# Key parts written once and spread by three transfers, a float32 head norm, and new prices in the planner

## The chip, the cores and the metric

The kernel runs on one core of a Trainium2 chip. The metric is the device time of one launch in microseconds (us). Before the change it is 791.28 us, the median of three runs between 790.02 and 792.25.

## The reference, cut to what matters

One layer of an encoder over two request groups that share weights: 1,040 prompt rows (16 meta tokens and 1,024 frames) and 32 sample rows with a cache of 272 rows. All of it is in float32.

```python
h = _rmsnorm(x, g)
z = h @ w_in                       # 1024 x 4104: dq, dk, dv, fq, fk, fv, forget logits, gate
...
sd = einsum(qd, Kd) * scale - slopes * dist      # 4 heads, two maps each
ad = softmax(sd)[:, :, 0] - lam * softmax(sd)[:, :, 1]
od = _rmsnorm(ad @ Vd, subln_g, 1e-5) * (1.0 - lam_init)     # the head norm, over 128 columns
...
of = softmax(einsum(qf, Kf) * scale + Fq - Fk) @ Vf          # 8 heads of 64
y = x + (concat(od, of) * silu(gate)) @ w_out
```

The new key and value rows and the forget logarithms are outputs as well, and y gets a last RMS norm.

## The kernel before, in words

**Number format.** TensorE works on float16 pairs: each float32 operand is split in a high part and a remainder (`hi`, `lo`), and a product is three products of the parts.

**Pairs.** The work is cut into eight pairs p of 128 columns. Pairs 0 to 3 are the four differential heads, whose 128 key columns are the two maps of 64; pairs 4 to 7 hold two forgetting heads of 64 each. For each pair there are projections of values, keys and queries (`proj_tasks`, the products of L864, in three column groups of up to 416, four for pair 0), then scores (`unit_tasks`, L1268), softmax (minimum on VectorE L1282, exponential on ScalarE L1288), splitting of the probabilities (L1317 to L1339, L1350, L1356), a transpose by DMA (L1368) and the products with the values (L1380 to L1387). The gate projections (also L864, weights `Wg`) come behind all pairs in priority and fill TensorE while the softmax of the pairs runs. At the end comes the output projection (L1806).

**Keys.** A projected group lies transposed on 128 partitions (`zT`, L883), map 0 on partitions 0 to 63 and map 1 on 64 to 127. The tile `k` is `[128, 2, 2, columns]`: map, then high part or remainder. A score product contracts 128 partitions: the query's high part on one half, its remainder on the other, against the same key on both halves. So the key of a map has to stand on both halves of the partitions. GpSimd writes the high part of each map on its own half (L891, two instructions a group), GpSimd or VectorE the remainder (L896, two a group; GpSimd for the pairs in `K_POOL`), and then one transfer per map copies the half to the other one (L993, 268 KB each, on SyncE's queue).

**Head norm.** `fin_tasks` normalizes the output of a differential head over its 128 rows, 256 columns at a time: sixteen times, and four times with 32 columns for the sample rows. ScalarE writes the values `o` and their squares `q`. For 256 columns GpSimd rounds the squares to float32r (L1441) and subtracts (L295, tile `fq`), and TensorE sums them over the partitions by two float32r products with a matrix of 1/128 (L1449, L1450); for 32 columns it is one float32 product (L1452). ScalarE takes r = exp(-0.5 ln(s + eps)) (L1457, L1458), and a Newton step sharpens it: VectorE v = (s + eps) r (L1463), GpSimd v = v r (L1470), VectorE v = (v - 3) r (L1474) and out = o v (L1475). The constants' signs are folded into the gain.

**Order.** Nothing is ordered at run time. A planner (`Graph.order`) simulates the engines as queues: each task has an engine, a cost in ns, a priority, the tasks it depends on and the buffers it takes; whenever an engine is free it takes the task of the highest priority whose buffers are there. The order that comes out is written down as each engine's instruction order. So a cost in a task changes no instruction, but where it stands. `c_dve`, `c_pool`, `c_act` and `c_mm` give costs by columns, `c_ts` that of a GpSimd tensor_scalar; a transfer is done 1,600 ns (`LANDED`) after its bytes, priced by `move` per KB, have moved.

```python
    def c_dve(n, k=1):
        return k * (165.0 + 1.08 * n)
    def c_ts(n):
        return 240.0 + 1.05 * n
```

In the functions printed here, `add(engine, cost, function, priority, dependencies, acquired, used)` makes a task.

Of the kernel before, what the change touches and what calls it, by code (L numbers as in the profile page):

```python
# [9 lines left out]
F32 = mybir.dt.float32  # L10
# [25 lines left out]
COLD = 3400.0  # L36

TRANSPOSED = 2000.0
LANDED = 1600.0
LATE = 8  # L40
# [20 lines left out]
FIN_POOL = True  # L61
# [200 lines left out]
def tile_hymba(  # L262
# [43 lines left out]

    def c_ts(n):
        return 240.0 + 1.05 * n
# [301 lines left out]
    def spread_task(col_, prio, deps):  # L610
# [12 lines left out]
        td = add("pool", 370, fd, prio, list(deps) + [cn["id"]], [dh])  # L623
# [22 lines left out]
    def w_tasks(key, prio):  # L646

        x = "Wg" if key[0] == "g" and key[1] < LATE else "W"
# [184 lines left out]
    def proj_tasks(kind, p, prio, step=0.1):  # L833
# [13 lines left out]
        for gi, (c0, c1) in enumerate(groups):  # L847
# [40 lines left out]
            if kind == "k":  # L888
                def fh(z=zT, c0=c0, c1=c1):
                    for m, (a, b) in enumerate(((0, 64), (64, 128))):  # L890
                        pool.tensor_scalar(out=K[p]["t"][a:b, m, 0, c0:c1], in0=z()[a:b], scalar1=1.0, scalar2=1.0,  # L891
                                           op0=ALU.mult, op1=ALU.mult)

                def fl(z=zT, c0=c0, c1=c1):
                    for m, (a, b) in enumerate(((0, 64), (64, 128))):
                        (pool if p in K_POOL else dve).tensor_tensor(  # L896
                            out=K[p]["t"][a:b, m, 1, c0:c1], in0=z()[a:b], in1=K[p]["t"][a:b, m, 0, c0:c1], op=ALU.subtract)
                th = add("pool", 2 * c_ts(n), fh, pr - 0.05, [tz], [], [zh, K[p]["hold"]])
                tl = add("pool" if p in K_POOL else "dve", c_pool(n, 2) if p in K_POOL else c_dve(n, 2), fl, pr, [th], [], [zh, K[p]["hold"]])
# [52 lines left out]
            if kind == "g":  # L952
# [29 lines left out]
                t4 = add("dve", c_dve(n, 2), f5, pr, [t4], [], [eh, ph])  # L982
                gate_done[p, gi] = dma(lambda p=p, c0=c0, c1=c1, n=n, loc=loc: sp.dma_start(
                    out=gate_s[128 * p:128 * p + 128, c0:c1], in_=loc["e"][:, :n]), pr, [t4], [], [eh], kb=n / 2)
        if kind == "k":
            K[p]["dup"] = []
            for i in range(2):
                b = 64 * i
                a = 64 - b

                def fd(i=i, a=a, b=b):
                    t = K[p]["t"]
                    sp.dma_start(out=t[a:a + 64, i], in_=t[b:b + 64, i])  # L993
                K[p]["dup"].append(dma(fd, prio, K[p]["hi"] + K[p]["lo"], [], [K[p]["hold"]], kb=268))
# [244 lines left out]
    def unit_tasks(p, hd, gg, prio, bias, av):  # L1239
# [5 lines left out]
        for bi in range(2):  # L1245
# [6 lines left out]
            for m in maps:  # L1252
# [44 lines left out]
                t = add("dve", 300, fq, prio + 0.3, [te, cn["lam"]])  # L1297
                if p < 4 and m == 1:
# [3 lines left out]
                    t = add("pool", 300 + 1.0 * nk, fp, prio + 0.3, [t], [], [ph])  # L1302
# [96 lines left out]
    def fin_tasks(p, get, ah, dep, n, d0, prio, u=1.0, ug=1.0):  # L1399
# [43 lines left out]
        if n > 32:  # L1443
            t1 = add("pool", c_ts(n) + c_pool(n), fs, prio, [t1], [], [fh])
# [506 lines left out]
```

## Time and profile before

| | |
|---|---|
| median of three runs | 791.28 us |
| the profiled execution | 794.14 us, its span 792.4 us |
| mean granted TensorE clock | 0.936 of full speed |
| busy: TensorE, VectorE, ScalarE, GpSimd | 684.0, 633.8, 498.9, 435.3 us |

The profile is one execution. The span runs from the first instruction to the last; the profiled execution's own time is longer by what lies around it. PE is TensorE, PEld its weight load, DVE is VectorE, ACT ScalarE, POOL GpSimd, and SP SyncE, which issues the transfers. A line such as L891 is a line of the kernel before. In a group of instructions the busy time is a sum over the whole span, the mean is that of one instruction, and the idle time is that of the engine just ahead of them, with what ended it. The chain is followed back from the last instruction to whatever released each step.

### The profile page before, as it was taken

What the parts mean: (1) busy time and instruction counts of PE and PEld (TensorE: products, weight loads), DVE (VectorE), ACT (ScalarE), POOL (GpSimd) and SP (SyncE); (2) the same over time, 40 slices, a digit from 0 to 9 for tenths busy, and PEclk for the clock granted to TensorE, in tenths of its full rate; (3) what the DMA queues carried; (4) which work ended last, traced back from release to release, by engine and by line L of the source; (5) the groups of instructions that cost most, each with busy time, mean ns of one, the idle gap of its engine ahead of it and who ended that gap; (6) DMA issues with size and microseconds to landing.
All of it is one profiled execution on the core that took longest, in us unless ns stands there. A gap on an engine that the chain in (4) does not pass through costs nothing.

```text
span 792.4 us, 14862 instructions
## 1 busy us (share of the span) xinstructions
PE 684.0 (86%) x4967; PEld 453.1 (57%) x4967; DVE 633.8 (80%) x1665; ACT 498.9 (63%) x1140; POOL 435.3 (55%) x606
## 2 busy tenths in 40 slices
PE   4477989898898899999899989979998973599996
PEld 4355565565765566666566667657665752334443
DVE  5966789888977889998889988878488889847643
ACT  4753578468766566876677677858488585434432
POOL 1447444698956569986867466546565148610000
PEclk8588999999899999999999999999999997599999
DMA  8284444556745355536686897788774987987611
GB/s 234 69 172 97 91 134 52 87 113 89 127 90 125 63 124 118 111 79 138 142 138 137 147 177 166 144 145 157 157 245 96 191 197 146 212 220 233 195 54 54
DMA packets 235804, 108.28 MB, mean 137 GB/s; under 512 B 149984, under 2 KB 228136, under 8 KB 235728
## 3 DMA queue, kind: packets, MB, share of 16 engines
q1 hardware_dynamic: 235728, 107.34, 62.9%
q8 instruction: 39, 0.64, 0.3%
q14 instruction: 37, 0.30, 0.1%
HBM read 46.39 MB, written 21.87 MB: 86 GB/s over the span
## 4 chain that ended last, share of the span: by engine, by line
PE 32%; DVE 16%; DMA 9%; POOL 6%; issue 4%; ACT 2%; SPq 1%; DVEq 0%; POOLq 0%; ACTq 0%
PE pj L864 13%; PE pj L1806 12%; DMA raw<-in_w_in_dram 4%; DMA arena<-arena 3%; DVE arena L1282 3%; DVE arena L1339 2%; PE sc L1268 2%; DMA ckr<-in_cache_diff_k_dram 2%; POOL k L896 1%; PE av L1384 1%; DVE gr L975 1%; PE av L1385 1%; DVE mx L1424 1%; POOL k L891 1%; DVE ge L971 1%
## 5 line engine op out<-in xcount | busy, mean ns | idle before, releaser
L864 PE MATMUL pj<-hT,W 128*128 128x384 f16 (+4 forms) x1776 | 294.9, 320 | 12.7 <-DVE ge L976 5.7
L864 PEld LDWEIGHTS <-W 128*128 128x128 f16 x1776 | 175.2, 101 | 110.7 <-issue 22.2
L1282 DVE CUSTOM_DVE_ANT_0 arena<-sc,G,stats 128x400 f32<-128x400 f32 (+9 forms) x224 | 128.6, 589 | 15.6 <-PE sc L1268 6.6
L1288 ACT ACTIVATE arena<-arena,stats 128x656 f32<-128x656 f32 (+7 forms) x128 | 99.9, 781 | 28.7 <-DVE stats L1282 26.8
L864 PE MATMUL pj<-hT,Wg 128*128 128x416 f16 (+2 forms) x576 | 97.6, 322 | 5.0 <-DVE ge L976 3.3
L1268 PE MATMUL sc<-k,q 128*128 128x400 f16 (+9 forms) x448 | 90.2, 311 | 8.1 <-DVE stats L1282 5.7
L1806 PE MATMUL pj<-hT,W 128*128 128x512 f16 (+4 forms) x440 | 95.6, 373 | 1.2 <-DVE W L1778 1.2
L618 POOL TENSOR_SCALAR diag<-ident,stats 128x128 bf16<-128x128 f32 x51 | 27.0, 529 | 99.9 <-ACT W L1773 48.5
L864 PEld LDWEIGHTS <-Wg 128*128 128x128 f16 x576 | 56.5, 101 | 35.5 <-issue 5.6
L1806 PEld LDWEIGHTS <-W 128*128 128x128 f16 (+2 forms) x440 | 41.7, 98 | 53.3 <-issue 8.6
L1384 PE MATMUL av<-arena,vn 128*128 128x128 f16 x288 | 43.3, 235 | 24.0 <-DMA arena<-arena 16.7
L1268 PEld LDWEIGHTS <-q 128*128 128x128 f16 x448 | 40.3, 100 | 29.5 <-issue 13.5
L1339 DVE SCALAR_TENSOR_TENSOR arena<-arena,stats 128x128 f16<-128x128 f32 (+4 forms) x80 | 50.5, 670 | 4.7 <-ACT arena L1331 3.7
L1356 POOL TENSOR_TENSOR arena<-arena 128x16 f16<-128x16 f32 (+3 forms) x48 | 36.3, 779 | 20.4 <-ACT arena L1350 20.3
L1323 POOL TENSOR_TENSOR arena<-arena 128x16 f16<-128x16 f32 (+7 forms) x56 | 44.1, 812 | 2.0 <-ACT arena L1317 1.9
L1385 PE MATMUL av<-arena,vn 128*128 128x128 f16 x288 | 43.4, 235 | 0.0
L883 ACT ACTIVATE zT<-pj 128x416 f32<-128x416 f32 (+4 forms) x50 | 22.5, 449 | 31.9 <-PE pj L864 30.8
L1385 PEld LDWEIGHTS <-vn 128*128 128x128 f16 x288 | 30.5, 106 | 18.7 <-issue 17.3
L1334 POOL TENSOR_SCALAR arena<-arena,stats 128x128 f16<-128x128 f32 (+2 forms) x32 | 22.9, 729 | 29.9 <-PE sc L1270 14.1
L1384 PEld LDWEIGHTS <-vn 128*128 128x128 f16 x288 | 30.6, 106 | 14.6 <-DVE mx L1424 7.7
L663 ACT ACTIVATE W<-raw 128x1024 bf16<-128x1024 f32 x24 | 25.2, 1050 | 19.8 <-DMA raw<-in_w_in_dram 19.6
L891 POOL TENSOR_SCALAR k<-zT 64x416 f16<-64x416 f32 (+4 forms) x50 | 30.1, 603 | 12.6 <-ACT zT L883 10.5
(318 smaller groups left out, 1566.5 us busy)
## 6 DMA issues: line engine op xcount, KB each, us to landing
raw<-in_w_in_dram SPq DMA_DIRECT2D x32, 512.0 KB
arena<-in_x_prompt_dram SPq DMA_DIRECT2D x16, 512.0 KB
k<-k SPq DMA_DIRECT2D x16, 268.0 KB
G<-G_t SPq DMA_DIRECT2D x8, 520.0 KB
mix_s<-mx SPq DMA_DIRECT2D x32, 128.0 KB
out_dram<-arena SPq DMA_DIRECT2D x16, 256.0 KB
arena<-mix_s SPq DMA_DIRECT2D x7, 512.0 KB
arena<-gate_s SPq DMA_DIRECT2D x7, 512.0 KB
```

Of the source, the lines that this page charges most:

```text
L618: pool.tensor_scalar(out=loc["d"], in0=ident, scalar1=col_, scalar2=1.0, op0=ALU.mult, op1=ALU.mult)
L864: mm(out, (W["hi"], W["hi"], W["lo"])[w][:, k, :], (hTh, hTl, hTh)[w][:, k, c0:c1], start=i == 0, stop=i == 23)
L891: pool.tensor_scalar(out=K[p]["t"][a:b, m, 0, c0:c1], in0=z()[a:b], scalar1=1.0, scalar2=1.0, op0=ALU.mult, op1=ALU.mult)
L1268: mm(s[:, :b - a], q, K[p]["t"][:, m, x, a:b], start=x == 0, stop=x == 1 and not mask)
L1282: dve.tensor_tensor_reduce(out=A(ph, nk)[:, a:b], in0=loc["s"][:, :b - a], in1=bl["t"][:, o + a:o + b], scale=Q[p]["tau"], scalar=3e38 if ...
L1288: te = add("act", c_act(nk) + 125, lambda ph=ph, nk=nk, mn=mn, sm=sm: act.activation(out=A(ph, nk), in_=A(ph, nk), func=AF.Exp, scale=-1.0 ...
L1323: (pool if on_pool else dve).tensor_tensor(out=A16(w, o, o + b - a), in0=x[:, a:b], in1=A16(w, h, h + b - a), op=ALU.subtract)
L1339: dve.scalar_tensor_tensor(out=A16(w, o, o + b - a), in0=x[:, a:b], scalar=rk, in1=A16(w, h, h + b - a), op0=ALU.mult, op1=ALU.subtract)
L1356: pool.tensor_tensor(out=A16(w, o, o + b - a), in0=x[:, a:b], in1=A16(w, h, h + b - a), op=ALU.subtract)
L1384: mm(out, vn[:, j, 128 * hd:128 * hd + 128], hi, start=j == 0, stop=False)
L1385: mm(out, vn[:, j, 128 * hd:128 * hd + 128], lw, start=False, stop=False)
L1806: mm(d, a, b, start=k == 0 and i == 0, stop=k == 7 and i == len(ops) - 1)
```

## The change

The diff, cut to its core:

```diff
+PORT = 200.0
+PORT_P = 150.0
-LATE = 8
+G_AT = (250, 260, 270, 280, 290, 300, 310, 320)
-FIN_POOL = True
...
+    def c_dvs(n, k=1):
+        return k * (PORT + 165.0 + 1.08 * n)
     def c_ts(n):
-        return 240.0 + 1.05 * n
+        return PORT_P + 240.0 + 1.05 * n
...
-        td = add("pool", 370, fd, prio, list(deps) + [cn["id"]], [dh])
+        td = add("pool", 370 + PORT_P, fd, prio, list(deps) + [cn["id"]], [dh])
...
                 def fh(z=zT, c0=c0, c1=c1):
-                    for m, (a, b) in enumerate(((0, 64), (64, 128))):
-                        pool.tensor_scalar(out=K[p]["t"][a:b, m, 0, c0:c1], in0=z()[a:b], scalar1=1.0, scalar2=1.0,
-                                           op0=ALU.mult, op1=ALU.mult)
+                    pool.tensor_scalar(out=K[p]["t"][:, 0, 0, c0:c1], in0=z(), scalar1=1.0, scalar2=1.0, op0=ALU.mult, op1=ALU.mult)
 
                 def fl(z=zT, c0=c0, c1=c1):
-                    for m, (a, b) in enumerate(((0, 64), (64, 128))):
-                        (pool if p in K_POOL else dve).tensor_tensor(
-                            out=K[p]["t"][a:b, m, 1, c0:c1], in0=z()[a:b], in1=K[p]["t"][a:b, m, 0, c0:c1], op=ALU.subtract)
-                th = add("pool", 2 * c_ts(n), fh, pr - 0.05, [tz], [], [zh, K[p]["hold"]])
-                tl = add("pool" if p in K_POOL else "dve", c_pool(n, 2) if p in K_POOL else c_dve(n, 2), fl, pr, [th], [], [zh, K[p]["hold"]])
+                    (pool if p in K_POOL else dve).tensor_tensor(
+                        out=K[p]["t"][:, 0, 1, c0:c1], in0=z(), in1=K[p]["t"][:, 0, 0, c0:c1], op=ALU.subtract)
+                th = add("pool", c_ts(n), fh, pr - 0.05, [tz], [], [zh, K[p]["hold"]])
+                tl = add("pool" if p in K_POOL else "dve", c_pool(n) if p in K_POOL else c_dvs(n), fl, pr, [th], [], [zh, K[p]["hold"]])
...
-            K[p]["dup"] = []
-            for i in range(2):
-                b = 64 * i
-                a = 64 - b
-
-                def fd(i=i, a=a, b=b):
-                    t = K[p]["t"]
-                    sp.dma_start(out=t[a:a + 64, i], in_=t[b:b + 64, i])
-                K[p]["dup"].append(dma(fd, prio, K[p]["hi"] + K[p]["lo"], [], [K[p]["hold"]], kb=268))
+            def fd1():
+                t = K[p]["t"]
+                sp.dma_start(out=t[64:128, 1], in_=t[64:128, 0])
+                sp.dma_start(out=t[0:64, 1], in_=t[64:128, 0])
+
+            def fd0():
+                t = K[p]["t"]
+                sp.dma_start(out=t[64:128, 0], in_=t[0:64, 0])
+            d1 = dma(fd1, prio, K[p]["hi"] + K[p]["lo"], [], [K[p]["hold"]], kb=536, move=2.25, n=2)
+            K[p]["dup"] = [dma(fd0, prio, [d1], [], [K[p]["hold"]], kb=268, move=2.25), d1]
...
-        def fs():
-            loc["qh"], loc["ql"] = [T([128, n], F32R, f"fq{i}") for i in range(2)]
-            pool.tensor_scalar(out=loc["qh"], in0=loc["q"], scalar1=1.0, scalar2=1.0, op0=ALU.mult, op1=ALU.mult)
-            sub_r(pool, loc["ql"], loc["q"], loc["qh"])
-        if n > 32:
-            t1 = add("pool", c_ts(n) + c_pool(n), fs, prio, [t1], [], [fh])
-
         def f2():
             loc["s"] = PSUM("sc")
-            if n > 32:
-                mm(loc["s"][:, :n], onesr, loc["qh"], start=True, stop=False)
-                mm(loc["s"][:, :n], onesr, loc["ql"], start=False, stop=True)
-            else:
-                mm(loc["s"][:, :n], onesm, loc["q"], start=True, stop=True)
-        t2 = add("pe", 2 * c_mm(n), f2, prio, [t1, cn["c"]], [sh], [fh])
+            mm(loc["s"][:, :n], onesm, loc["q"], start=True, stop=True)
+        t2 = add("pe", 4 * c_mm(n), f2, prio, [t1, cn["c"]], [sh], [fh])
...
         def f5():
-            v, r0 = loc["v"], loc["r"]
-            loc["mx"] = T([128, n], F32, x + "mx", RINGS[x + "mx"])
-            (pool if FIN_POOL else dve).tensor_tensor(out=v, in0=v, in1=r0, op=ALU.mult)
-
-        def f6():
-            v, r0 = loc["v"], loc["r"]
-            dve.scalar_tensor_tensor(out=v, in0=v, scalar=-3.0, in1=r0, op0=ALU.add, op1=ALU.mult)
-            dve.tensor_tensor(out=loc["mx"], in0=loc["o"], in1=v, op=ALU.mult)
-        t5 = add("pool" if FIN_POOL else "dve", c_pool(n) if FIN_POOL else c_dve(n), f5, prio, [t4], [mh], [fh])
-        t5 = add("dve", c_dve(n, 2), f6, prio, [t5], [], [fh, mh])
+            pool.tensor_tensor(out=loc["o"], in0=loc["o"], in1=loc["r"], op=ALU.mult)
+            pool.tensor_tensor(out=loc["v"], in0=loc["v"], in1=loc["r"], op=ALU.mult)
+
+        def f6():
+            loc["mx"] = T([128, n], F32, x + "mx", RINGS[x + "mx"])
+            dve.scalar_tensor_tensor(out=loc["mx"], in0=loc["v"], scalar=-3.0, in1=loc["o"], op0=ALU.add, op1=ALU.mult)
+        t5 = add("pool", c_pool(n, 2), f5, prio, [t4], [], [fh])
+        t5 = add("dve", c_dvs(n), f6, prio, [t5], [mh], [fh])
```

The high part and the remainder of both maps are now written by one instruction each, into the place of map 0. Two transfers then copy partitions 64 to 127, which are map 1, into the place of map 1 on both halves; after they have landed, a third copies map 0 over partitions 64 to 127 of its own place. The head norm uses one float32 product for all sizes, and its last step is out = (v r - 3) (o r).

Not shown are the other places where the planner's price of a task is changed: `c_dvs` (200 ns more an instruction) replaces `c_dve` for the gates' last two VectorE steps (L975, L976), for the sum of the two maps (L1312) and for the remainders of the probabilities on VectorE (L1323, L1339); the reciprocals of L1292 get 80 ns more; the scaling of L1300 is priced by `c_ts`, as are the others of that kind. `G_AT` replaces the formula for the gates' priorities, which gave 250 to 320 as well, and with `LATE` at 8 every gate weight already used the ring `Wg`.

## Rows read from the trace of the kernel before

**Rows 1.** Page of the profile, part 1: busy us, share of the span, instructions by engine.

```profile
PE 684.0 (86%) x4967; PEld 453.1 (57%) x4967; DVE 633.8 (80%) x1665; ACT 498.9 (63%) x1140; POOL 435.3 (55%) x606
```

**Rows 2.** Stretches: from:to, length, PE, PEld, DVE, ACT, POOL busy us (count), clock, DMA, GB/s.

```profile
100.00:410.00 310.00, 280.22 (x2127) 192.68 (x2126) 270.76 (x743) 215.68 (x524) 226.44 (x307) 0.96 0.55 107
410.00:580.00 170.00, 159.37 (x1281) 110.55 (x1280) 138.63 (x402) 117.97 (x267) 100.71 (x158) 0.99 0.80 153
580.00:640.00 60.00, 56.12 (x451) 38.24 (x449) 52.25 (x158) 46.68 (x108) 21.68 (x31) 0.97 0.78 193
640.00:690.00 50.00, 25.38 (x223) 18.68 (x221) 45.15 (x102) 31.34 (x60) 37.10 (x31) 0.78 0.79 160
```

**Rows 3.** Timeline of TensorE, the last gate projection: start, length, what.

```profile
644.64 1.57 PE L864 MATMUL pj<-hT,Wg 128*128 128x416 f16 x8
```

**Rows 4.** Waits of TensorE from 640 to 690 us: total us, times, longest.

```profile
PE av L1384 <- DMA arena<-arena: 10.6, 5, 4.2
PE av L1384 <- DVE mx L1424: 7.3, 2, 4.1
```

**Rows 5.** Page, part 4: the chain that ended last, by engine and by line.

```profile
PE 32%; DVE 16%; DMA 9%; POOL 6%; issue 4%; ACT 2%; SPq 1%; DVEq 0%; POOLq 0%; ACTq 0%
PE pj L864 13%; PE pj L1806 12%; DMA raw<-in_w_in_dram 4%; DMA arena<-arena 3%; DVE arena L1282 3%; DVE arena L1339 2%; PE sc L1268 2%; DMA ckr<-in_cache_diff_k_dram 2%; POOL k L896 1%; PE av L1384 1%; DVE gr L975 1%; PE av L1385 1%; DVE mx L1424 1%; POOL k L891 1%; DVE ge L971 1%
```

**Rows 6.** Groups by line, the key parts: count | busy us, mean ns | idle before.

```profile
L896 POOL TENSOR_TENSOR k<-zT,k 64x272 f16<-64x272 f32 (+2 forms) x36 | 34.3, 954 | 2.7
...
L891 POOL TENSOR_SCALAR k<-zT 64x416 f16<-64x416 f32 (+4 forms) x50 | 30.1, 603 | 12.6 <-ACT zT L883 10.5
...
L896 DVE TENSOR_TENSOR k<-zT,k 64x256 f16<-64x256 f32 (+4 forms) x14 | 8.4, 600 | 3.3 <-POOL k L891 3.1
```

**Rows 7.** Instructions of L891: min/median/max ns.

```profile
L891 POOL TENSOR_SCALAR k<-zT x50: 302/530/1982, 67.2 to 569.0; 64x416 f16<-64x416 f32 x16, 64x272 f16<-64x272 f32 x14, 64x384 f16<-64x384 f32 x14, 64x256 f16<-64x256 f32 x4
```

**Rows 8.** Instructions on tile fs: min/median/max ns.

```profile
L1441 POOL TENSOR_SCALAR fq<-fs x16: 394/406/1367, 132.9 to 405.2; 128x256 fp32r<-128x256 f32 x16
...
L1463 DVE SCALAR_TENSOR_TENSOR fs<-sc,fr x16: 401/421/426, 144.7 to 409.6; 128x256 f32<-128x256 f32 x16
...
L1474 DVE SCALAR_TENSOR_TENSOR fs<-fs,fr x16: 406/426/1569, 151.3 to 411.2; 128x256 f32<-128x256 f32 x16
L1475 DVE TENSOR_TENSOR mx<-ft,fs x16: 424/515/2237, 152.7 to 411.6; 128x256 f32<-128x256 f32 x16
```

**Rows 9.** Groups by line: the head norm, and float32 products of the warm-up.

```profile
L295 POOL TENSOR_TENSOR fq<-fs,fq 128x256 fp32r<-128x256 f32 x16 | 14.2, 888 | 1.3
...
L1470 POOL TENSOR_TENSOR fs<-fs,fr 128x256 f32<-128x256 f32 x16 | 13.5, 846 | 8.3 <-DVE fs L1463 8.1
L1475 DVE TENSOR_TENSOR mx<-ft,fs 128x256 f32<-128x256 f32 x16 | 13.4, 839 | 0.5
...
L1441 POOL TENSOR_SCALAR fq<-fs 128x256 fp32r<-128x256 f32 x16 | 11.0, 688 | 5.0 <-ACT fs L1435 4.8
...
L1474 DVE SCALAR_TENSOR_TENSOR fs<-fs,fr 128x256 f32<-128x256 f32 x16 | 10.8, 676 | 4.2 <-POOL fs L1470 4.1
...
L1864 PE MATMUL pj<-ident 128*128 128x128 f32 x48 | 7.5, 333 | 1.4 <-POOL eps L1855 1.4
```

**Rows 10.** Timeline of TensorE, one head norm's pair, then the next product.

```profile
164.98 0.36 PE L1449 MATMUL sc<-fq,onesr 128*128 128x256 f32 x1
165.18 0.28 PE L1450 MATMUL sc<-fq,onesr 128*128 128x256 f32 x1
165.29 0.30 PE L1452 MATMUL sc<-sfs,onesm 128*128 128x32 f32 x2
```

**Rows 11.** Chain in order of time, pair 7: start, us, what.

```profile
576.54 3.10 DMA k<-k
```

**Rows 12.** Waits of TensorE over the span, on the key transfers: total us, times, longest.

```profile
PE sc L1268 <- DMA k<-k: 0.2, 1, 0.2
```

**Rows 13.** Timeline of TensorE, the first score of pair 7.

```profile
579.68 0.28 PE L1268 MATMUL sc<-k,q 128*128 128x144 f16 x2 [0.22 <-DMA k<-k]
```

More of the change, by code (lines that the diff above doesn't have):

```diff
@@ L646, in w_tasks @@
     def w_tasks(key, prio):
-        x = "Wg" if key[0] == "g" and key[1] < LATE else "W"
+        x = "Wg" if key[0] == "g" else "W"
         rh, wh = Hold("raw"), Hold(x)
@@ L981, in proj_tasks @@
                          [t3], [], [eh])
-                t4 = add("dve", c_dve(n, 2), f5, pr, [t4], [], [eh, ph])
+                t4 = add("dve", c_dvs(n, 2), f5, pr, [t4], [], [eh, ph])
                 gate_done[p, gi] = dma(lambda p=p, c0=c0, c1=c1, n=n, loc=loc: sp.dma_start(
@@ L1296, in fq @@
                         dve.tensor_tensor(out=rk, in0=r, in1=lam3[1], op=ALU.mult)
-                t = add("dve", 300, fq, prio + 0.3, [te, cn["lam"]])
+                t = add("dve", 300 + 0.4 * PORT, fq, prio + 0.3, [te, cn["lam"]])
                 if p < 4 and m == 1:
@@ L1301, in fp @@
                                            op0=ALU.mult, op1=ALU.mult)
-                    t = add("pool", 300 + 1.0 * nk, fp, prio + 0.3, [t], [], [ph])
+                    t = add("pool", c_ts(nk), fp, prio + 0.3, [t], [], [ph])
                 rec[m] = (t, r, rk)
@@ L1312, in fc @@
                     dve.scalar_tensor_tensor(out=P0, in0=P0, scalar=rk, in1=A(P[1], nk), op0=ALU.mult, op1=ALU.add)
-                t = add("dve", c_dve(nk), fc, prio + 0.3, [rec[0][0], rec[1][0]], [], [P[0], P[1]])
+                t = add("dve", c_dvs(nk), fc, prio + 0.3, [rec[0][0], rec[1][0]], [], [P[0], P[1]])
                 def fh(nb=nb, w=w, ph=P[0], nk=nk):
@@ L1361, in unit_tasks @@
             on_pool = on_pool if p < 4 else full
-            tl = add("pool" if on_pool else "dve", c_pool(nb) + 170 if on_pool else c_dve(nb) + 150, fl, prio + 0.2, [th], [], [w, P[m]])
+            tl = add("pool" if on_pool else "dve", c_pool(nb) + 170 if on_pool else c_dvs(nb) + 150, fl, prio + 0.2, [th], [], [w, P[m]])
             z = Hold("arena", nb + 64)
@@ L1896, in tile_hymba @@
             continue
-        if kind == "g" and p >= LATE:
-            proj_tasks(kind, p, FILL + 10 * (idx - p + LATE) + p - LATE, 3.0)
+        if kind == "g":
+            proj_tasks(kind, p, FILL + G_AT[p])
         else:
-            proj_tasks(kind, p, FILL + 10 * idx if p or kind == "g" else FIRST[kind])
+            proj_tasks(kind, p, FILL + 10 * idx if p else FIRST[kind])
         if kind == "q":
```

## The prediction

> **What bounds the kernel now.** I read four views, from the coarse to the fine. The page's first part [rows 1] shows TensorE at 86% and VectorE at 80% of the span, with GpSimd at 55%. These are averages over unlike stages, so the second view is the busy time by stretch [rows 2]. From 100 to 640 us TensorE has 310 - 280.2, 170 - 159.4 and 60 - 56.1 us idle: 44.3 us in 540. VectorE is at 87% in the first of these stretches and GpSimd at 73%. From 640 to 690 us the picture turns over: VectorE has 45.2 of 50 us, TensorE 25.4, at a granted clock of 0.78. This is a drain. The last gate projection, the work that fills TensorE while softmax runs, starts at 644.64 us [rows 3]; after it TensorE waits for transposed probabilities and for the heads' last VectorE step [rows 4]. So the time is made of TensorE's work, 44 us of small gaps, and a drain whose length VectorE sets. The third view is the waits just named, the fourth the chain that ended last [rows 5]: 32% TensorE, 16% VectorE, 6% GpSimd. L891 and L896, which the change halves, lie on it with about 1% each, 7.9 us of 792.4 each.
>
> **The change part by part.** The sum is made on the profiled execution: 794.14 us, of which 792.4 is the span. It stands 2.86 us above the median of 791.28, and I carry the difference over unchanged.
>
> *Key parts in one instruction.* The 50 roundings of L891 on GpSimd become 25, the 36 subtractions on GpSimd become 18 and the 14 on VectorE 7 [rows 6]. An instruction over 128 partitions has to cost what one over 64 did. Rows bear that out: on 64 partitions L891 takes 302 ns at its shortest, pair 0's group of 144 columns, and 530 at the median, which falls among those of 384 [rows 7]. A straight line through the two gives 408 ns at 256 columns; L1441, the same operation on 128 partitions, takes 406 at the median [rows 8]. So 15.05 + 17.15 = 32.2 us leave GpSimd and 4.2 us leave VectorE. Of this the chain holds about 15.8 us, and half is 7.9. A shortened chain is soon replaced by what is late next, here the projection behind it on TensorE's queue, so I count three quarters: **-5.9 us**. The ends are 0 (all of it was cover) and -15.8 (twice the share, as the rounded 1% could hide more).
>
> *Head norm on GpSimd and VectorE.* For 16 groups of 256 columns the rounding and the subtraction go (11.0 + 14.2 us), and one multiplication of L1470's size comes (13.5 us) [rows 9]. GpSimd saves 11.7 us, less four small multiplications for the sample rows, each below 0.85 us. VectorE loses L1475's sixteen instructions, 13.4 us, and four small ones. In all GpSimd sheds about 43 us and VectorE 17.6. The norm's own chain loses a step ahead of TensorE of 0.69 + 0.89 us, and behind it swaps 0.84 us on VectorE for 0.85 us on GpSimd. Nothing waits for its end before the output projection, so this latency is worth nothing by itself; the work it hides behind is the next pair's projections. Its ends are 0 and -13.4.
>
> *Contention.* L1463, with one operand in PSUM, takes 401 to 426 ns. L1474 and L1475, with both operands in SBUF, have the same floor and reach 1,569 and 2,237 [rows 8]; their means are 270 and 415 ns above their fastest [rows 9]. So VectorE's two-SBUF-operand instructions lose time to something beside them, and GpSimd is what the change thins out: 43 of the 327 us it is busy from 100 to 580 us, 13%. L1474's 16 lose 4.3 us. I estimate some 160 instructions of that kind in the stretch at the same 270 ns, 43 us, and 13% of that is 5.6 us. VectorE is the second engine, so a third of it: **-1.9 us**, ends 0 and -5.6.
>
> The Trainium skill, "SBUF — State Buffer", section "SBUF: two separate sides", states that GpSimd and a VectorE instruction with two SBUF inputs take one port pair in turns, and the loser waits for the whole instruction. That speaks against the added multiplication, which by that rule could hold VectorE 16 x 0.85 = 13.6 us at worst; it speaks for the removed ones as well. The trace agrees in the spread of L1475.
>
> *The float32 product.* Two rounded products of 256 columns now take from 164.98 to 165.29 us: 0.31 us of TensorE [rows 10]. The new one is one float32 product. The warm-up's 24 float32 products of 128 columns take 7.5 us as 48 records, 0.31 each [rows 9]. For 256 columns that bounds it: 0.31 if loading the weights set the pace, 0.62 if the columns did. I take the middle, 0.47: 16 x 0.16 = **+2.5 us**, ends 0 and +5.0. TensorE has no cover for it.
>
> The Trainium skill, "FP8 and Floating Point Precision", section "TensorE Precision Notes", gives true float32 four passes. With the 0.11 us of L1450 that is 0.44 us, and the sum would have +2.1.
>
> *Three transfers.* Map 1 is put in place and copied; only when that has landed is map 0 spread, so a second transfer stands in a row. One lasts 3.10 us from issue to landing [rows 11], and with a half microsecond of issue for the extra one, map 0 comes 3.6 us later. In the whole trace TensorE waited for such a transfer once, 0.2 us [rows 12]. That was pair 7, whose first score at 579.68 us started as map 0 landed [rows 13]: there it lies on the chain. The other seven pairs are covered by the projections that stand before their first scores, and where map 1 is there first its scores can go ahead. **+3.6 us**, ends 0 and 8 x 3.6 = +28.8; the second is far off, since only one of eight waited at all. While SyncE waits 3.1 us for the landing, the probability transposes queue behind it, and the output products of L1384 would wait for those, 8 x 3.1 = 24.8 us if nothing else were put there. The planner prices this landing at 1,206 + 1,600 + 300 ns, which is 3.1 us, so it can put other issues in between.
>
> *The planner's prices.* GpSimd's tensor_scalar gains 150 ns in the plan, some VectorE instructions 200, so every engine's order moves. Nothing in the trace prices it. Its bounds are the 44.3 us of gaps on one side (I let it close a quarter, -11) and on the other side a longer drain, +12 (below). I take 0. The gates' new start numbers equal the old.
>
> Sum: -5.9 - 1.9 + 2.5 + 3.6 = -1.7 us from what can be placed on the path. The relief of VectorE, 17.6 us, is not in it beyond that. It bears on the drain: where softmax runs ahead, gate projections are left to fill the 24.6 us that TensorE idles there. A third of 17.6, by the weight of VectorE beside TensorE on the chain (16 to 32), is **-5.9**. Together -7.6: 786.5 in this execution, **783.7 us** as a median.
>
> **The rivals.** *The relief closes the drain.* All 17.6 us of VectorE count, with the placed -1.7: 772. For it: VectorE is 90% busy in the drain. Against: the gates themselves need VectorE.
>
> *TensorE is the bound.* Relief lands where there was room, and only the placed terms stay, with the key parts at half their credit: about -1.7 + 3 = +1.3 to -1.7, 789.6 to 792.6. For it: TensorE at 94% from 410 to 640 us.
>
> *The plan spends the gates too early.* With dearer VectorE steps the planner sees softmax as slower and puts more gate work between its scores. The raised prices of the late half (24 gate tasks by 400 ns, some 40 subtractions by 200) come to 9.6 + 8 = 17.6 us of planned VectorE time. If two thirds of that, 12 us (TensorE's part of the 32 and 16 on the chain), is filled with gate projections ahead of time, the drain grows by as much, and against the gain of 7.6 the time is 795.7. It decides once the last gate product ends some 8 us earlier against the end of the drain than now. For it: the drain exists already. Against: measured VectorE steps are longer than their minimum, so the dearer plan is the truer one.
>
> *The halving does not hold* (128 partitions dearer) is priced by the first term's end, 0: 789.6; [rows 7, 8] speak against it.
>
> **How the numbers follow.** Forecast 0.46, its own range 779 to 788.5; drain closed 0.14; TensorE bound, with the halving failed, 0.16; gates spent early 0.24. Some 0.3%, 2.4 us, is about what a measurement of this kernel can tell from no change. Faster takes the first two, 0.60; same 0.15; slower 0.25, with a little of the third. The range takes in most of all four: 773 to 798.
>
> **What would show it.** L891 and L896 at half their counts and unchanged means; L1475 gone, GpSimd near 392 us and VectorE below 616; the float32 product at 0.44 to 0.5 us; TensorE's idle from 100 to 640 below 40 us; a drain shorter than 50. It is wrong if pair 7's first scores leave TensorE waiting over 4 us, or if the last gate projection ends earlier against the drain's end.

## The result: slower by 3.7%, with less work done

The changed kernel takes 821.76 us, the median of four runs (816.15 to 823.2), beside 791.76 us for the kernel before: a ratio of 1.0366, with a 95% interval from 1.0313 to 1.042. That is 30 us where I had forecast a gain of 7.6. The profiled execution has a span of 821.5 us, against 792.4.

The first part of the changed kernel's page, beside [rows 1]:

```profile
PE 695.6 (85%) x4967; PEld 458.1 (56%) x4967; DVE 603.3 (73%) x1638; ACT 499.6 (61%) x1140; POOL 389.6 (47%) x551
```

VectorE is busy 30.5 us less and GpSimd 45.7 us less; TensorE 11.6 us more, in a span 29.1 us longer. TensorE's instructions are as many as before, 4,967, and its mean granted clock is 0.915 where it was 0.936; how much of the 11.6 us comes from the clock was not isolated. So no engine has become the bound by added work, and 29.1 - 11.6 = 17.5 us are new idle time of TensorE.

The groups of instructions by line (count | busy us, mean ns of one | idle before) answer to [rows 6, 9]. L895 and L898 are L891 and L896 of before, L1446 is the float32 product, L1462 and L1463 are the two multiplications on GpSimd, L1467 is the last step on VectorE:

```profile
L898 POOL TENSOR_TENSOR k<-zT,k 128x272 f16<-128x272 f32 (+2 forms) x18 | 16.1, 892 | 1.5
...
L1463 POOL TENSOR_TENSOR fs<-fs,fr 128x256 f32<-128x256 f32 x16 | 14.8, 924 | 2.5 <-DVE sfs L1457 2.3
...
L895 POOL TENSOR_SCALAR k<-zT 128x416 f16<-128x416 f32 (+4 forms) x25 | 13.8, 553 | 22.3 <-ACT zT L888 22.2
...
L1462 POOL TENSOR_TENSOR ft<-ft,fr 128x256 f32<-128x256 f32 x16 | 11.8, 737 | 8.5 <-ACT fr L1452 8.2
...
L1467 DVE SCALAR_TENSOR_TENSOR mx<-fs,ft 128x256 f32<-128x256 f32 x16 | 11.4, 713 | 1.1 <-POOL fs L1463 1.0
...
L1446 PE MATMUL sc<-fs,onesm 128*128 128x256 f32 x32 | 9.9, 391 | 0.6 <-ACT fs L1440 0.6
```

The key parts did what the change says: half the counts, and means of 553 and 892 ns where 603 and 954 stood. The loss lies elsewhere. The busy time by stretch (length, then busy us and count of PE, PEld, DVE, ACT, POOL; granted clock, DMA share, GB/s), beside [rows 2]:

```profile
100.00:410.00 310.00, 278.25 (x2061) 188.05 (x2060) 239.37 (x695) 205.93 (x499) 186.94 (x258) 0.96 0.54 105
410.00:580.00 170.00, 153.67 (x1222) 107.96 (x1221) 127.58 (x379) 116.44 (x264) 84.64 (x131) 0.96 0.75 153
580.00:640.00 60.00, 57.61 (x491) 40.34 (x489) 49.55 (x159) 45.50 (x106) 29.77 (x53) 1.00 0.87 189
640.00:690.00 50.00, 32.16 (x247) 22.04 (x244) 42.10 (x122) 33.61 (x73) 16.83 (x23) 0.78 0.86 197
690.00:740.00 50.00, 31.41 (x146) 14.90 (x147) 31.40 (x49) 17.95 (x31) 26.04 (x19) 0.64 0.60 154
```

From 100 to 640 us TensorE idles 31.8 + 16.3 + 2.4 = 50.5 us, 6.2 more than before. VectorE, at 87% in the first stretch before, is at 77%: some of its work is gone, and it waits longer. Its costliest group, the minimum over the scores, does as much work as before and waits more than twice as long ahead of it, first the kernel before, then the changed one:

```profile
L1282 DVE CUSTOM_DVE_ANT_0 arena<-sc,G,stats 128x400 f32<-128x400 f32 (+9 forms) x224 | 128.6, 589 | 15.6 <-PE sc L1268 6.6
L1287 DVE CUSTOM_DVE_ANT_0 arena<-sc,G,stats 128x400 f32<-128x400 f32 (+7 forms) x224 | 128.9, 590 | 36.8 <-PE sc L1273 19.9
```

By 640 us TensorE has 2,061 + 1,222 + 491 = 3,774 matmul records since 100, against 3,859 [rows 2]. Then comes a drain as before, but longer. TensorE's last gate projection and its first product of the output projection in the changed kernel's timeline (start, length, engine, line; in brackets what it idled for):

```profile
660.62 2.98 PE L869 MATMUL pj<-hT,Wg 128*128 128x416 f16 x16
```

```profile
713.36 0.26 PE L627 MATMUL tr<-diag,onesb 128*128 128x128 bf16 x1 [11.93 <-POOL diag L623]
...
716.07 2.16 PE L1798 MATMUL pj<-hT,W 128*64 128x512 f16 x4 [1.14 <-DVE W L1770]
```

The gate's last products begin at 660.62 and last 2.98 us, to 663.6; before it was 644.64 + 1.57 = 646.2 [rows 3]. The output projection begins at 716.07; in the kernel before it began at 688.58:

```profile
688.58 2.17 PE L1806 MATMUL pj<-hT,W 128*64 128x512 f16 x4 [1.16 <-DVE W L1778]
```

So 17.4 us are lost before the gates end, and the drain, from there to the output projection, grew from 42.4 to 52.5 us. What TensorE waited for from 640 to 720 us (total, times, longest), beside [rows 4]:

```profile
PE av L1389 <- DMA arena<-arena: 15.0, 5, 7.5
PE tr L627 <- POOL diag L623: 13.0, 2, 11.9
```

The 11.93 us wait is for a small spreading step on GpSimd (L623), the first output scale. GpSimd's and VectorE's timelines show what stood before it:

```profile
705.46 2.29 POOL L1705 TENSOR_TENSOR hT<-arena,hT 128x1024 f16<-128x1024 f32 x1 [0.76 <-ACT hT L1703]
708.77 2.12 POOL L1705 TENSOR_TENSOR hT<-raw,hT 128x1024 f16<-128x1024 f32 x1 [1.02 <-ACT hT L1703]
710.87 2.09 POOL L1712 TENSOR_SCALAR hT<-raw,stats 128x1024 f16<-128x1024 f32 x1
712.94 2.02 POOL L623 TENSOR_SCALAR diag<-ident,stats 128x128 bf16<-128x128 f32 x3
```

```profile
688.79 1.33 DVE L1751 TENSOR_TENSOR arena<-arena 128x1024 f32<-128x1024 f32 x1 [0.72 <-DMA arena<-gate_s]
...
705.70 3.14 DVE L1751 TENSOR_TENSOR arena<-arena 128x1024 f32<-128x1024 f32 x1
708.76 4.22 DVE L1344 SCALAR_TENSOR_TENSOR arena<-arena,stats 128x1024 f16<-128x1024 f32 x2
```

GpSimd's queue holds three steps on the output weights (L1705, L1712) ahead of L623, and VectorE's steps beside them are stretched: L1751 takes 1.33 us at 688.79 and 3.14 us at 705.70. In the kernel before, the output weights came earlier against the drain, with 37.1 us of GpSimd's time from 640 to 690 [rows 2], and TensorE's longest wait in this stretch was 4.2 us [rows 4].

### The profile page after: what moved, and what is told of

It is laid out like the page before. It is cut to its first block, busy times and chain, and to the rows that moved or that the text cites. A ratio compares the mean times of both kernels' runs of the same rounds, so it can differ in the third digit from the quotient of the medians.

```text
span 821.5 us, 14756 instructions
## 1 busy us (share of the span) xinstructions
PE 695.6 (85%) x4967; PEld 458.1 (56%) x4967; DVE 603.3 (73%) x1638; ACT 499.6 (61%) x1140; POOL 389.6 (47%) x551
## 4 chain that ended last, share of the span: by engine, by line
PE 30%; DMA 16%; DVE 12%; ACT 9%; issue 4%; SPq 2%; POOL 1%; DVEq 0%; ACTq 0%; POOLq 0%
PE pj L1798 11%; DMA arena<-arena 11%; PE pj L869 10%; DMA raw<-in_w_in_dram 2%; PE sc L1273 2%; ACT arena L1293 2%; DVE arena L1344 2%; DVE arena L1287 2%; DMA k<-k 1%; PE av L1389 1%; PE av L1390 1%; DVE ge L964 1%; DVE W L689 1%; ACT arena L1336 1%; ACT q L929 1%
## 5 line engine op out<-in xcount | busy, mean ns | idle before, releaser
L869 PE MATMUL pj<-hT,W 128*128 128x384 f16 (+4 forms) x1776 | 298.2, 322 | 8.3 <-DVE ge L978 4.7
L1287 DVE CUSTOM_DVE_ANT_0 arena<-sc,G,stats 128x400 f32<-128x400 f32 (+7 forms) x224 | 128.9, 590 | 36.8 <-PE sc L1273 19.9
L1293 ACT ACTIVATE arena<-arena,stats 128x272 f32<-128x272 f32 (+7 forms) x128 | 99.8, 780 | 27.0 <-DVE stats L1287 26.1
L1273 PE MATMUL sc<-k,q 128*128 128x400 f16 (+7 forms) x448 | 92.8, 321 | 10.2 <-DVE stats L1287 9.6
L869 PE MATMUL pj<-hT,Wg 128*128 128x416 f16 (+2 forms) x576 | 95.3, 319 | 3.3 <-DVE ge L978 2.9
L623 POOL TENSOR_SCALAR diag<-ident,stats 128x128 bf16<-128x128 f32 x51 | 28.1, 552 | 119.8 <-ACT W L1765 49.6
L869 PEld LDWEIGHTS <-Wg 128*128 128x128 f16 x576 | 56.1, 99 | 33.5 <-issue 5.8
L1389 PE MATMUL av<-arena,vn 128*128 128x128 f16 x288 | 44.7, 238 | 29.2 <-DMA arena<-arena 28.0
L1328 POOL TENSOR_TENSOR arena<-arena 128x16 f16<-128x16 f32 (+7 forms) x56 | 47.6, 872 | 21.4 <-ACT arena L1322 17.8
L1344 DVE SCALAR_TENSOR_TENSOR arena<-arena,stats 128x128 f16<-128x128 f32 (+4 forms) x80 | 46.9, 632 | 0.7 <-ACT arena L1336 0.4
L1390 PE MATMUL av<-arena,vn 128*128 128x128 f16 x288 | 45.0, 239 | 0.0
L1305 POOL TENSOR_SCALAR arena<-arena,stats 128x144 f32<-128x144 f32 (+7 forms) x32 | 33.1, 1038 | 18.5 <-DVE stats L1297 13.4
L668 ACT ACTIVATE W<-raw 128x1024 bf16<-128x1024 f32 x24 | 25.2, 1050 | 26.9 <-DMA raw<-in_w_in_dram 26.7
L934 DVE SCALAR_TENSOR_TENSOR q<-pj,q 64x256 f16<-64x256 f32 (+2 forms) x48 | 25.0, 522 | 20.7 <-ACT q L929 13.1
```

What stands on the lines that cost most here:

```text
L623: pool.tensor_scalar(out=loc["d"], in0=ident, scalar1=col_, scalar2=1.0, op0=ALU.mult, op1=ALU.mult)
L869: mm(out, (W["hi"], W["hi"], W["lo"])[w][:, k, :], (hTh, hTl, hTh)[w][:, k, c0:c1], start=i == 0, stop=i == 23)
L1273: mm(s[:, :b - a], q, K[p]["t"][:, m, x, a:b], start=x == 0, stop=x == 1 and not mask)
L1287: dve.tensor_tensor_reduce(out=A(ph, nk)[:, a:b], in0=loc["s"][:, :b - a], in1=bl["t"][:, o + a:o + b], scale=Q[p]["tau"], scalar=3e38 if ...
L1293: te = add("act", c_act(nk) + 125, lambda ph=ph, nk=nk, mn=mn, sm=sm: act.activation(out=A(ph, nk), in_=A(ph, nk), func=AF.Exp, scale=-1.0 ...
L1305: pool.tensor_scalar(out=A(ph, nk), in0=A(ph, nk), scalar1=r, scalar2=lam3[2], op0=ALU.mult, op1=ALU.mult)
```

## The experiments

All times are medians with the kernel before run beside them; the ratios are to it, with 95% intervals. For a version that re-plans the old or new parts, the price formula of L1300 stays the old one where the GpSimd price is 0.

**Order or instructions?** The first two kernels cross the two. In one, the tasks, costs and dependencies that the planner sees are those before, so the written order is the old one, and only the functions emit the new instructions. The cut shows what differs from the change's own functions:

```diff
 def fd(i=i):                 # task of map i, in the old plan
+    if K[p]["spread"]: return
+    K[p]["spread"] = True
     t = K[p]["t"]
-    sp.dma_start(out=t[a:a + 64, i], in_=t[b:b + 64, i])
+    sp.dma_start(out=t[64:128, 1], in_=t[64:128, 0])
+    sp.dma_start(out=t[0:64, 1], in_=t[64:128, 0])
+    sp.dma_start(out=t[64:128, 0], in_=t[0:64, 0])
...
 def fs():                    # rounding of the squares
+    pass
```

> The order of the instructions is that of the kernel before, with the new instructions put in their places: key parts in one instruction each, all three transfers at the place of the first, the float32 product, the new Newton step. If the order is what costs (my theory), this stands at 780 to 793 us, since less work is done in the same order. If the new instructions cost (the row of two transfers with SyncE waiting between them, or the float32 product), it stands at 805 to 825.

Measured: 798.41 us, 1.0103 (1.0051 to 1.0156). It lies between my two cases. With the new instructions in both, the change's order takes 23 us more than the old one, so the order makes up most of the 30 us; but the new parts, put into an order that was not planned for them, lose 8 us. The waits of SyncE's queue and of TensorE on the key transfers in this run:

```profile
SPq L993 <- DMA k<-k: 30.6, 10, 4.7
```

```profile
PE sc L1268 <- DMA k<-k: 9.7, 4, 3.0
```

In the other kernel the changed kernel's order emits the old instructions, with the rounding of the squares placed right ahead of the product:

```diff
 def f2():
+    pool.tensor_scalar(out=qh, in0=loc["q"], ...); sub_r(pool, ql, loc["q"], qh)
-    mm(loc["s"][:, :n], onesm, loc["q"], start=True, stop=True)
+    mm(loc["s"][:, :n], onesr, qh, ...); mm(loc["s"][:, :n], onesr, ql, ...)
```

> The order is that of the changed kernel, with the old instructions put in their places: two instructions a key part, one transfer a map, the rounded products, the old Newton step. If the order costs, 820 to 835 us, as the changed kernel or somewhat slower for the added GpSimd and VectorE work. If the new instructions cost, 785 to 800.

Measured: 849.16 us, 1.075 (1.0699 to 1.0801), above my window. The order is slow with either set of instructions. The size says little of the old parts, since TensorE now waits for a rounding that this plan had no room for:

```profile
PE sc L1452 <- POOL fq L1450: 18.8, 12, 4.7
```

**Prices or tasks?** The next two split what changed the order.

```diff
 # the kernel before, all prices as in the change, no other edit
+PORT = 200.0
+PORT_P = 150.0
```

> The kernel before with the new prices in the planner alone, and so another order of the same instructions. If the prices alone spoil the order, 810 to 825 us. If the order is spoilt by the changed tasks (three transfers in a row, the shorter norm), 785 to 797.

Measured: 808.85 us, 1.0227 (1.0186 to 1.0268): the same instructions in another order, and 18.5 us more, just below my window for a spoilt order.

```diff
 # the changed kernel
-PORT = 200.0
-PORT_P = 150.0
+PORT = 0.0
+PORT_P = 0.0
```

> The changed kernel with the planner's old prices (both additions at 0). If the prices alone spoil the order, 780 to 793 us. If the changed tasks do, 805 to 825, as the changed kernel.

Measured: 800.68 us, 1.0124 (1.0089 to 1.0159), between my two windows. The new tasks and instructions with the old prices cost 10 us, the prices alone 18.5, both 30. That looks like a sum, but the later runs show that it is not one.

**The norm and the keys apart,** each in the old order, with the edits shown above.

> The order of the kernel before, with the new head norm alone in its places; keys as before. The norm sheds GpSimd and VectorE work and adds 2.5 us of TensorE by my estimate. If the loss of 8 us with both new parts in the old order comes from the keys' row of transfers, this stands at 784 to 791 us. If the float32 product or the two multiplications on GpSimd cost, at 793 to 800.

Measured: 788.57 us, 0.9974 (0.995 to 0.9999), in the first window. The norm alone is at most a small gain, its interval ending just below 1, and it is the one version here whose interval lies below the kernel before. The first part of its page:

```profile
PE 684.5 (87%) x4967; PEld 453.2 (58%) x4967; DVE 625.6 (79%) x1645; ACT 498.9 (63%) x1140; POOL 427.6 (54%) x594
```

VectorE is 8.2 us below [rows 1], where the prediction had 13.4; GpSimd is 7.7 below, where it had 11.7; TensorE is 0.5 above.

> The order of the kernel before, with the key parts in one instruction and all three transfers at the place of the first; norm as before. If the row of transfers costs, 796 to 804 us, with SyncE waiting some 30 us for landings and TensorE some 10 for the keys, as with both parts. If it does not, 784 to 792.

Measured: 800.67 us, 1.0124 (1.0083 to 1.0165), in the window of a cost. The row of transfers costs when nothing is put between its two steps. TensorE's waits on the keys in this run:

```profile
PE sc L1268 <- DMA k<-k: 7.4, 3, 3.0
```

Pair 0 in this run's timeline, SyncE's queue and then TensorE's first score:

```profile
97.96 0.54 SPq L991 DMA_DIRECT2D k<-k  x1
98.55 0.59 SPq L992 DMA_DIRECT2D k<-k  x1
102.38 0.46 SPq L993 DMA_DIRECT2D k<-k  x1
```

```profile
105.42 0.42 PE L1268 MATMUL sc<-k,q 128*128 128x144 f16 x2 [3.00 <-DMA k<-k]
```

The third transfer could be issued only at 102.38 us, the first having gone out at 97.96, and the score began at 105.42 after 3.00 us of waiting.

**What a price means.** If the plan had become worse because dearer VectorE steps say something, a tiny price would change little.

```diff
 # the kernel before
+PORT = 10.0
+PORT_P = 0.0
```

> The instructions of the kernel before, and the VectorE prices raised by 10 ns instead of 200, the GpSimd prices not at all. As a statement about the chip this says next to nothing. If a price matters by what it says (dearer VectorE steps, more gate work ahead), it stays within 788 to 793 us. If any other order than the one found costs, because the order before was a lucky one among many, it stands at 797 to 815.

Measured: 813.84 us, 1.0295 (1.0257 to 1.0334). Ten nanoseconds on a planned cost, no instruction changed, 23 us. TensorE's wait for the spreading steps in this run's last stretch (640 to 760 us) has one of 26.9 us:

```profile
PE tr L628 <- POOL diag L624: 30.8, 3, 26.9
```

Still, the drain in which that wait stands takes 44.2 us, only 1.8 more than in the kernel before, so most of the loss lies ahead of it.

```diff
 # the kernel before
+PORT = 0.0
+PORT_P = 10.0        # 6.0 for the scaling of L1300
```

> The instructions of the kernel before, and the GpSimd prices raised by 10 ns (of the scaling of the second map by 6) instead of 150, the VectorE prices not at all. By the theory of a price's meaning 788 to 793 us; by the theory of a lucky order 797 to 815.

Measured: 808.11 us, 1.0211 (1.0181 to 1.0242). Both stand where the theory of a lucky order put them. That a tiny price costs doesn't show that a large one has no effect by its meaning; the table of drains below bears on that.

**The same for the new parts.** The prices 10 and 0, then 190 and 150, in the changed kernel:

> The changed kernel's instructions, planned with the old prices but 10 ns more on the VectorE steps. With the old prices it took 800.7 us. If the spread between orders is luck, this lies anywhere from 798 to 825 us and most likely some per cent away from 800.7; if the prices act by their meaning, it stays at 798 to 803.

Measured: 794.22 us, 1.0032 (1.0012 to 1.0052), below the windows of both theories: another order, and here a better one.

> The changed kernel with 190 ns in place of 200 as the VectorE price. If the spread between orders is luck, it is away from 821.8 us by more than 5 us, within 798 to 830; if high prices cost by their meaning, 818 to 825.

Measured: 795.83 us, 1.006 (1.0033 to 1.0087): far from 821.8, as the theory of luck had it, but below the window of that theory as well. One price 5% lower, and 26 of the 30 us are gone. The last stretches of this run, its last gate projection and its first full output product:

```profile
580.00:640.00 60.00, 54.72 (x426) 37.78 (x426) 46.98 (x139) 44.54 (x103) 19.05 (x33) 0.94 0.86 202
640.00:690.00 50.00, 21.45 (x179) 15.14 (x177) 40.59 (x73) 26.92 (x46) 35.14 (x23) 0.71 0.90 214
690.00:740.00 50.00, 48.09 (x202) 19.60 (x203) 27.25 (x69) 18.68 (x40) 5.04 (x8) 0.94 0.42 129
```

```profile
652.19 1.57 PE L869 MATMUL pj<-hT,Wg 128*128 128x416 f16 x8
```

```profile
692.18 1.04 PE L1798 MATMUL pj<-hT,W 128*128 128x512 f16 x2 [0.58 <-ACT W L1768]
```

The gates end at 653.8 us, 9.8 earlier than in the changed kernel, and the output product that stands here begins 38.4 us later. GpSimd does its 35.1 us of work from 640 to 690, as the kernel before did (37.1), where the changed kernel did 16.8 there and 26.0 after.

**The keys in the order of the changed kernel,** with two instructions a part and one transfer a map:

```diff
-    sp.dma_start(out=t[64:128, 1], in_=t[64:128, 0])
-    sp.dma_start(out=t[0:64, 1], in_=t[64:128, 0])
+    sp.dma_start(out=t[0:64, 1], in_=t[64:128, 1])
```

> The order of the changed kernel with two instructions a key part and one transfer a map, as before; the new norm stays. In this order TensorE waits 0.3 us for key transfers, so the row of transfers is covered where it is planned for. If the one-instruction keys help by the GpSimd time they free, this is slower than the changed kernel: 823 to 832 us. If the row of transfers still costs through SyncE, it is faster: 810 to 819.

Measured: 825.91 us, 1.0446 (1.041 to 1.0483), against 1.0366 (1.0313 to 1.042) for the changed kernel: the two intervals overlap by 0.1%. So the new keys don't cost in an order that plans for them. That they gain is not shown: the difference is 4 us by the medians, and the old keys stand here in an order that was not planned for them, as the new ones did in the old order.

**Is it GpSimd's queue in the drain?** A part of the output weights' computation is left out. Both cut steps work on 16 of 1,024 columns, as the rows below show of the second; the "quarter" in the expectation is an error:

```diff
-    pool.tensor_scalar(out=lw["raw"], in0=lw["raw"], scalar1=sco, ...)
+    pool.tensor_scalar(out=lw["raw"][:, 0:16], in0=lw["raw"][:, 0:16], scalar1=sco, ...)
...
-    pool.tensor_tensor(out=part(1, al), in0=raw(), in1=part(0, al), op=ALU.subtract)
+    pool.tensor_tensor(out=part(1, al)[:, :, 0:2], in0=raw()[:, :, 0:2], in1=part(0, al)[:, :, 0:2], op=ALU.subtract)
```

> The changed kernel's order, with GpSimd's scaling and remainder of four of the eight output-weight blocks cut to a sixty-fourth and a quarter of their columns (a part of that computation is left out). In the changed kernel GpSimd works at these until 713 us, the spreading of the first output scale stands behind them, and TensorE waits 11.9 us for it, while VectorE's steps beside them take up to twice their time. If this queue is what lengthens the drain, the time falls by 8 to 15 us, to 807 to 814. If the drain hangs on the probabilities' transposes alone, by less than 4.

Measured: 817.39 us, 1.0365 (1.0302 to 1.0428). That is the changed kernel's ratio, and 4.4 us less by the medians; the window of 8 to 15 us is missed. With the work cut, GpSimd stands idle in the same place, and L623 still comes late.

```profile
700.21 1.18 POOL L1705 TENSOR_TENSOR hT<-arena,hT 128x16 f16<-128x16 f32 x1 [7.92 <-ACT hT L1703]
703.52 0.24 POOL L1705 TENSOR_TENSOR hT<-raw,hT 128x16 f16<-128x16 f32 x1 [2.13 <-ACT hT L1703]
...
704.84 2.02 POOL L623 TENSOR_SCALAR diag<-ident,stats 128x128 bf16<-128x128 f32 x3
```

It idles 7.92 and 2.13 us for ScalarE's copies ahead of the shortened steps, and L623 follows in the same order. The copies in turn stand in ScalarE's order behind the exponential of a late score, L1293 at 696.89 us, ahead of which ScalarE idled 6.63 us for VectorE. So mainly it is not the amount of GpSimd's work that holds the spreading step back, but what stands ahead of it in the written order and what that waits for. In this execution, the fastest of its four, the drain is 48.4 us (659.56 to 707.98) against 52.5, so up to 4 us may hang on the amount.

**Neighbours of the changed prices.** Four more orders, each planned afresh. The first two and the last are the changed kernel at (200, 140), (210, 150) and (5, 0), prices for VectorE and GpSimd; the third is the old parts at (190, 150):

> The changed kernel with 140 ns in place of 150 as the GpSimd price. Four plans of the new parts took 794.2, 795.8, 800.7 and 821.8 us. If 821.8 is one bad order among many, this stands at 790 to 806; if prices near 200 and 150 are bad by their meaning and 190 was the exception, at 812 to 828.

Measured: 806.38 us, 1.0158 (1.0102 to 1.0214); just above my window.

> The changed kernel with 210 ns in place of 200 as the VectorE price. One bad order among many: 790 to 806. Prices bad by their meaning: 812 to 828.

Measured: 808.81 us, 1.0209 (1.0167 to 1.0251); it falls between the windows.

> The old parts with the prices 190 and 150. Three new orders of the old parts took 808 to 814 us. If the new parts are the cheaper ones once the order is drawn anew for both, this stands at 803 to 818, above the 795.8 of the new parts at the same prices. If there is no such gain, at 790 to 800.

Measured: 799.09 us, 1.008 (1.0049 to 1.0112); below the window of a gain, above the new parts' 795.83.

> The changed kernel with the old prices and 5 ns more on the VectorE steps. Another draw of an order for the new parts: 790 to 806 us by the theory of luck. Should it fall below 788, it beats both kernels.

Measured: 790.47 us, 0.9982 (0.9961 to 1.0004): the same as the kernel before.

All orders planned afresh, medians in us:

| prices (VectorE, GpSimd) | old parts | new parts |
|---|---|---|
| 0, 0 | the kernel before: 790.4 to 792.6 | 800.7 |
| 5, 0 | | 790.5 |
| 10, 0 | 813.8 | 794.2 |
| 0, 10 | 808.1 | |
| 190, 150 | 799.1 | 795.8 |
| 200, 140 | | 806.4 |
| 200, 150 | 808.9 | the change: 821.8 |
| 210, 150 | | 808.8 |

The seven plans of the new parts have a mean of 802.6 us and spread over 31; the four re-planned ones of the old parts a mean of 807.5, over 15. At equal prices the new parts win at (10, 0) and (190, 150) and lose at (0, 0) and (200, 150). The times follow no clear trend in the prices. The changed kernel is the slowest plan of its own parts, and the kernel before stands below every other plan of its parts that was run.

**Where the plans lose their time** can be read from their traces: how many of the 576 gate products TensorE had done by 580 us, when the last of them ended, when the output projection began, and the drain between the two. Each row is one profiled execution.

| prices | parts | gate products by 580 us | gates end, us | output begins, us | drain, us |
|---|---|---|---|---|---|
| 0, 0 | old (before) | 312 | 646.2 | 688.6 | 42.4 |
| 10, 0 | old | 336 | 664.2 | 708.4 | 44.2 |
| 0, 10 | old | 288 | 664.2 | 702.5 | 38.3 |
| 190, 150 | old | 408 | 639.2 | 695.3 | 56.1 |
| 200, 150 | old (prices alone) | 432 | 646.1 | 704.2 | 58.1 |
| 0, 0 | new | 277 | 664.5 | 695.1 | 30.6 |
| 5, 0 | new | 384 | 636.1 | 685.9 | 49.8 |
| 10, 0 | new | 312 | 651.7 | 690.6 | 38.9 |
| 190, 150 | new | 336 | 653.8 | 692.2 | 38.4 |
| 200, 140 | new | 344 | 647.3 | 696.0 | 48.7 |
| 200, 150 | new (the change) | 408 | 663.6 | 716.1 | 52.5 |
| 210, 150 | new | 336 | 646.8 | 703.0 | 56.2 |

TensorE's busy time on the gate weights (tile `Wg`) in the first 580 us, for the kernel before, the prices alone and the change (busy us and count, then granted clock, DMA share, GB/s), and the last gate projection and the first output product of the prices alone:

```profile
0.00:580.00 580.00, 51.86 (x312) 0.94 0.63 125
0.00:580.00 580.00, 73.34 (x432) 0.94 0.60 125
0.00:580.00 580.00, 66.39 (x408) 0.93 0.61 125
```

```profile
644.55 1.57 PE L870 MATMUL pj<-hT,Wg 128*128 128x416 f16 x8
704.18 2.16 PE L1812 MATMUL pj<-hT,W 128*64 128x512 f16 x4 [3.07 <-DVE W L1784]
```

From the first output product to the end, all twelve take 101.7 to 105.4 us, so what a plan costs is there when that product begins. It is lost in two places. With the new prices alone the gates end when they did before, and the whole loss is in the drain, 15.7 us longer: TensorE had given 73.3 us to gate products by 580 us instead of 51.9, and these were then missing where they would have filled the drain. The old parts at (190, 150) show the same. A nudge of 10 ns leaves the drain of the old parts near what it was, and the gates end 18 us later. Over all twelve, more gate products ahead of 580 us mostly go with a longer drain, but not always: (190, 150) and (210, 150) with the new parts have 336 each, and drains of 38.4 and 56.2 us.

## Why the prediction was wrong

**The step that failed** is the term for the planner's prices: "I take 0", with ends of -11 and +12. Measured alone it is +18.5 us (808.85 against 790.35), outside both ends. In the traces this is the longer drain that the upper end stood for, +15.7 us. The working lacked a second effect: any touch re-draws the order, and the old order was not one of many equal ones, so that even 10 ns cost 17 to 23 us. The new tasks re-draw it as well: with the old prices the changed kernel takes 800.68 us, with 5 ns more 790.47.

**The key parts,** -5.9: the GpSimd time fell as worked out (64.4 us of [rows 6] became 29.9, so 34.5 against 32.2 forecast), but re-planned, its share of the time can't be told from the re-drawn order. In the changed order the swap back to the old keys and transfers cost 4 us, at the edge of the intervals.

**The three transfers,** +3.6: the mechanism was right, the size hung on the order. In the old order, with nothing between, the new keys as a whole cost 9.9 us, and TensorE waited 7.4 us for them at three scores, the first of pair 0 among them, where I had called the first seven pairs covered. Where the planner knew of them SyncE waited 9.2 us instead of some 30, so other issues went in between, as the prediction supposed. The changed kernel's waits of SyncE and of TensorE for them, the second beside [rows 12]:

```profile
SPq L997 <- DMA k<-k: 9.2, 5, 3.4
```

```profile
PE sc L1273 <- DMA k<-k: 0.3, 1, 0.3
```

**The float32 product,** +2.5: one takes 0.43 us, from 150.24 to 150.67, where the pair took 0.31 [rows 10], so +1.9 us for sixteen. The Trainium skill, "FP8 and Floating Point Precision", section "TensorE Precision Notes", has four passes for it; the prediction's estimate from that, 0.44 us and +2.1, came nearer than my middle of two bounds.

```profile
150.24 0.59 PE L1446 MATMUL sc<-fs,onesm 128*128 128x256 f32 x2
150.67 1.57 PE L869 MATMUL pj<-hT,W 128*128 128x416 f16 x8
```

**The norm on VectorE** was right in sign as far as can be told: alone, in the old order, 0.26% faster, at the edge of its interval. It shed 8.2 us of VectorE, not 13.4.

**Contention,** -1.9: VectorE sheds 30.5 us in the changed kernel, where 17.6 + 5.6 = 23.2 were forecast. But the order alone moves this figure: the same new parts in the old order have VectorE busy 612.6 us, 21.2 less than before, and the old parts with the new prices alone 626.4, 7.4 less. So the amount was about right, and what it is worth in time can't be told from these runs; in the changed kernel VectorE spent it waiting, as the rows of L1287 show.

**The drain term,** -5.9, went the other way: the drain grew by 10 us. *The plan spends the gates too early* was the rival nearest to it. Its sign, and its test of 8 us against the drain's end, held, and its cause is borne out for this part. By 580 us the changed kernel had done 96 gate products more than before, 14.5 us of TensorE's time by the busy times above, while from 100 to 580 us all its products together were 125 fewer (3,283 against 3,408): the pairs' own products stood some 220 behind, and the gates that should fill the drain were spent. With the prices alone it was 120 gate products and 21.5 us, and a drain of 58.1. I had this rival at +12 and a chance of 0.24. It is not the whole loss: 17.4 of the 27.5 us up to the output projection were lost before the gates ended, 190 ns, which say nearly the same as 200, left the new parts a drain of 38.4, and the nudges of 10 ns cost as much with no longer drain. What exactly in the order costs those 17.4 us was not isolated; the idle time is spread over many waits. Of the signs named in the prediction, the busy times of GpSimd (389.6) and VectorE (603.3) came in, the float32 product just missed its range, and TensorE's idle time from 100 to 640 us, 50.5 where below 40 was forecast, missed; the second sign of being wrong, an earlier end of the gates against the drain's end, came true.

## What to carry to other kernels

When a change touches anything that a planner reads, measure the order apart from the instructions: emit the new instructions in the old order, and the old ones under a cost moved by a few nanoseconds. If a meaningless nudge moves the time by more than the change should, one measurement of the changed kernel says little about the change; compare several plans of each version, and keep the best. And look in each plan at when the work that fills the waits of others runs out. Time freed on engines off the bound is worth little (the norm's 8 us on each of two engines gave 0.26%, hardly clear of nothing), and a transfer that waits for another holds its queue unless the plan has work to put there.

## What the runs showed of the hardware

VectorE's L1751, a product of two SBUF operands of 1,024 columns, took 1.33 us at 688.79 and 3.14 us at 705.70, in the rows above. Both times it began within a GpSimd step, and both times it ended 1.1 us after that step did: L1705 ran to 707.75 and L1751 to 708.84; in the earlier case GpSimd's step ended at 689.05 and L1751 at 690.12:

```profile
687.77 1.28 POOL L1701 TENSOR_SCALAR stv<-stv,stats 128x1024 f32<-128x1024 f32 x1
```

The kernel before shows it once more: the same step, L1759 there, ran from 679.00 to 681.06, and GpSimd's L1709 had ended at 679.99. The median of this step is 1.2 us in either kernel. So the three cases fit a step that waited for GpSimd's to end and then took about its usual time, and not one that ran slowly beside it. The Trainium skill, "SBUF — State Buffer", section "SBUF: two separate sides", says that the loser of the shared port pair blocks for the whole instruction, and the trace agrees in these three.

A GpSimd instruction over 128 partitions cost about what one over 64 did: at the median 510 ns against 530 for the rounding and 917 against 912 for the subtraction, at the mean 553 against 603 and 892 against 954.
